# Rotary embedding on one core: casting transfers of every fourth partition with 16 KB rows, and 4,096-wide VectorE operations

## The chip, the cores and the metric

The kernel runs on one core of one Trainium2 chip. Its time is the device time of an execution in microseconds (us); for the kernel before it is 168.24 us, the median of two runs that agree. The profile is of one execution, and its span, from the first to the last instruction, is 166.5 us.

Five kinds of engine matter little or much here: VectorE (DVE in the profile) does all the arithmetic, GpSimd (POOL) issues all large transfers, SyncE (SP) issues two small ones, and the core's 16 DMA engines move the data between the chip's memory (HBM) and the on-chip memory of 128 partitions (SBUF). TensorE and ScalarE do nothing.

## The reference

Each row of 1,024 numbers is cut into 16 heads of 64, and each head into two halves of 32. The halves are rotated by tables that depend on the position in the sequence:

```python
batch, seq, dim = 16, 512, 1024          # x: float32, 33.55 MB
num_heads = 16                           # head_dim = 64, half_dim = 32
x1, x2 = x[..., :half_dim], x[..., half_dim:]
cos = cos[None, :, None, :]              # cos, sin: (512, 32)
sin = sin[None, :, None, :]
rotated = np.concatenate([
    x1 * cos - x2 * sin,
    x1 * sin + x2 * cos,
], axis=-1)                              # float32, 33.55 MB
```

## The kernel before

Each of the 128 partitions holds four neighbouring positions of a batch entry (`spp = 4`). A chunk is two of these positions for all partitions: 128 x 2,048 elements, 8 KB of float32 for each partition. There are 32 chunks. GpSimd's loads cast float32 to bf16 on the way into SBUF, its stores cast bf16 to float32 on the way out.

```python
spp = seq // P                 # 4
rows = 2
W = rows * dim                 # 2048
per_batch = spp // rows        # 2
nchunks = batch * per_batch    # 32
ahead = 6
xpool: bufs=ahead + 3;  tpool: bufs=3;  opool: bufs=6

def dram(t, c):
    b, k = divmod(c, per_batch)
    return bass.AP(tensor=t.tensor,
                   offset=t.offset + b * seq * dim + k * rows * dim,
                   ap=[[spp * dim, P], [1, W]])

def load(c):
    xb = xpool.tile([P, W], bf16, tag="xb")
    nc.gpsimd.dma_start(out=xb, in_=dram(x, c))
    return xb
# ... cos and sin are loaded by SyncE, the first `ahead` chunks by GpSimd;
# ... VectorE makes the bf16 tables cc = [cos, cos] and ss = [sin, -sin]

for c in range(nchunks):
    # ...
    for j in range(rows):          # operations of 1,024 elements
        nc.vector.tensor_mul(out=row(t1), in0=row(xb), in1=tab(cc))
        nc.vector.tensor_mul(out=row(t2), in0=row(xb), in1=tab(ss))
        # swapped: t2 with the two halves of each head exchanged
        nc.vector.tensor_add(out=row(ot), in0=row(t1), in1=swapped)
    nc.gpsimd.dma_start(out=dram(out_flat, c), in_=ot)
    if c + ahead < nchunks:
        xbs[c + ahead] = load(c + ahead)
```

`tab(t)` reads a row of 64 table entries 16 times over, once for each head. In GpSimd's order each store is followed by the load of the chunk six further on.

## Time and profile before

| | |
|---|---|
| Time | 168.24 us |
| Span of the profiled execution | 166.5 us |
| VectorE busy | 120.1 us (72%), 195 instructions |
| GpSimd busy | 34.5 us (21%), 68 instructions |
| Loads issued by GpSimd | 32, each 512 KB as written to SBUF (1 MB as read) |
| Stores issued by GpSimd | 32, each 1,024 KB as written to HBM |
| Mean of one VectorE operation of 1,024 elements | 0.684 to 0.687 us |
| Mean of one DMA issue on GpSimd | 0.538 us |

The profile's page shows, for each engine, how much of the span it was busy, and the same in 40 equal slices, in which a digit 9 stands for 90% or more. A row for the DMA engines stands beside them. The chain of waits starts from the last instruction and steps back, each time to whatever released it, so its shares say what the end of the kernel hung on. The table of groups has one line per kind of instruction: how many, their busy time, the mean duration in ns, and behind the last bar the idle time of the engine just ahead of them and what ended it. VectorE's operations overlap a little: each is 0.68 us long, but one starts every 0.60 us when nothing holds it.

Sizes of transfers are given as written, so a load counts half of what it reads from HBM. The trace also has a record of every packet that a DMA engine handled, with its start, duration and size as written. One row of one partition is one packet.

### The profile page before, as it was taken

The numbers are of one execution on the slowest core, as the hardware profiler recorded it, in microseconds if no ns is written. First come the engines' busy times: TensorE is split into PE (matmuls) and PEld (weight loads), VectorE is DVE, ScalarE is ACT, GpSimd is POOL, SyncE is SP. The second block draws the span as 40 slices with busy tenths as digits, with TensorE's granted clock in tenths as the row PEclk, the third lists the DMA queues.
The fourth block names the chain that finished last, engine by engine and source line by source line (L and its number), as shares of the span: only waits on it lengthen the run. The fifth ranks groups of instructions, "written<-read, shape, count | busy, mean of one in ns | idle before, by whom it ended". The sixth has DMA issues, their size and how long they took to land.

```text
span 166.5 us, 365 instructions
## 1 busy us (share of the span) xinstructions
DVE 120.1 (72%) x195; POOL 34.5 (21%) x68
## 2 busy tenths in 40 slices
DVE  1399999998778878777987777797775987775000
POOL 7123222222212212221221221221221211111000
DMA  4999999999999999999999999999999999999980
GB/s 74 203 217 208 270 299 302 324 341 340 326 303 297 311 334 342 338 312 303 299 322 337 342 333 301 303 302 336 337 340 318 299 303 314 341 371 431 429 333 2
DMA packets 9507, 50.49 MB, mean 303 GB/s; under 512 B 1056, under 2 KB 1312, under 8 KB 5408
## 3 DMA queue, kind: packets, MB, share of 16 engines
q0 software_dynamic: 9216, 50.34, 104.1%
q1 hardware_dynamic: 288, 0.13, 0.3%
q14 instruction: 3, 0.02, 0.0%
HBM read 33.69 MB, written 33.55 MB: 404 GB/s over the span
## 4 chain that ended last, share of the span: by engine, by line
DMA 72%; issue 9%; DVE 9%; POOL 1%; POOLq 0%; DVEq 0%; PEldq 0%
DMA xb<-in_x_dram 72%; DVE t L95 3%; DVE ot L100 3%; DVE t L96 3%; POOL out_dram L101 1%; POOLq L134 0%; POOLq L101 0%; DVEq L95 0%; PEldq L134 0%
## 5 line engine op out<-in xcount | busy, mean ns | idle before, releaser
L95 DVE TENSOR_TENSOR t<-xb,cc 128x1024 bf16<-128x1024 bf16 x64 | 44.0, 687 | 28.8 <-DMA xb<-in_x_dram 28.8
L100 DVE TENSOR_TENSOR ot<-t,t 128x1024 bf16<-128x1024 bf16 x64 | 43.9, 686 | 0.7
L96 DVE TENSOR_TENSOR t<-xb,ss 128x1024 bf16<-128x1024 bf16 x64 | 43.8, 684 | 0.0
L101 POOL DMA_DIRECT2D out_dram<-ot x32 | 17.2, 538 | 85.0 <-DMA out_dram<-ot 42.2
L52 POOL DMA_DIRECT2D xb<-in_x_dram x32 | 17.1, 539 | 33.3 <-DMA xb<-in_x_dram 32.5
L68 DVE CAST cc<-cos_sb 128x256 bf16<-128x256 f32 x1 | 0.3, 294 | 2.6 <-DMA cos_sb<-in_cos_dram 2.6
L76 DVE CAST ss<-sin_sb 128x128 bf16<-128x128 f32 x1 | 0.2, 227 | 0.1
L77 DVE TENSOR_SCALAR ss<-sin_sb 128x128 bf16<-128x128 f32 x1 | 0.2, 220 | 0.0
L120 POOL MEMSET const-float32-0.0<- 128x1 f32 x1 | 0.1, 99 | 0.2 <-issue 0.2
L120 POOL MEMSET const-bfloat16-1.0<- 128x1 bf16 x1 | 0.1, 102 | 0.0
L120 POOL MEMSET const-float32-1.0<- 128x1 f32 x1 | 0.1, 99 | 0.0
L120 POOL MEMSET const-uint8-127<- 128x1 uint8 x1 | 0.1, 99 | 0.0
## 6 DMA issues: line engine op xcount, KB each, us to landing
out_dram<-ot POOLq DMA_DIRECT2D x32, 1024.0 KB, 19.1
xb<-in_x_dram POOLq DMA_DIRECT2D x32, 512.0 KB, 19.3
cos_sb<-in_cos_dram SPq DMA_DIRECT2D x1, 64.0 KB, 1.8
sin_sb<-in_sin_dram SPq DMA_DIRECT2D x1, 64.0 KB, 1.8
```

The lines of the kernel that those rows point to most:

```text
L52: nc.gpsimd.dma_start(out=xb, in_=dram(x, c))
L68: nc.vector.tensor_copy(out=cc, in_=dataclasses.replace(cos_sb, ap=[cos_sb.ap[0], [half, spp], [0, 2], [1, half]]))
L76: nc.vector.tensor_copy(out=ss_half(0), in_=sin_rows)
L77: nc.vector.tensor_scalar_mul(out=ss_half(1), in0=sin_rows, scalar1=-1.0)
L95: nc.vector.tensor_mul(out=row(t1), in0=row(xb), in1=tab(cc))
L96: nc.vector.tensor_mul(out=row(t2), in0=row(xb), in1=tab(ss))
L100: nc.vector.tensor_add(out=row(ot), in0=row(t1), in1=swapped)
L101: nc.gpsimd.dma_start(out=dram(out_flat, c), in_=ot)
L120: nc = _bacc.Bacc("TRN2", target_bir_lowering=False, num_devices=1)
```

## The change

A chunk becomes all four positions of a partition, 128 x 4,096 elements, so a row is 16 KB of float32 and there are 16 chunks. Each chunk is moved by four transfers; transfer `r` takes partitions `r, r+4, r+8, ...`, which are 32 rows. In GpSimd's order, store `r` of a chunk is followed by load `r` of the chunk three further on, so that stores and loads alternate in pieces of 512 KB at the float32 side. Three chunks are loaded ahead, the same number of bytes as six of the chunks before.

VectorE makes both products and the sum of a chunk in one operation each, 4,096 elements wide. The purpose is fewer and larger packets, a finer alternation of loads and stores, and fewer VectorE instructions.

```diff
-    rows = 2
+    rows = 4
     W = rows * dim
     per_batch = spp // rows
     nchunks = batch * per_batch
-    ahead = 6
+    ahead = 3
+    pstep = 4
...
-    xpool = ctx.enter_context(tc.tile_pool(name="xpool", bufs=ahead + 3))
+    xpool = ctx.enter_context(tc.tile_pool(name="xpool", bufs=ahead + 1))
     tpool = ctx.enter_context(tc.tile_pool(name="tpool", bufs=3))
-    opool = ctx.enter_context(tc.tile_pool(name="opool", bufs=6))
+    opool = ctx.enter_context(tc.tile_pool(name="opool", bufs=4))
...
-    def dram(t, c):
+    def dram(t, c, r):
         b, k = divmod(c, per_batch)
         return bass.AP(tensor=t.tensor,
-                       offset=t.offset + b * seq * dim + k * rows * dim,
-                       ap=[[spp * dim, P], [1, W]])
+                       offset=t.offset + b * seq * dim + r * spp * dim + k * W,
+                       ap=[[pstep * spp * dim, P // pstep], [1, W]])
...
+    def load(c, r):
+        if r == 0:
+            xbs[c] = xpool.tile([P, W], bf16, tag="xb", name="xb")
+        nc.gpsimd.dma_start(out=xbs[c][r::pstep, :], in_=dram(x, c, r))
+
+    def store(c, r, ot):
+        nc.gpsimd.dma_start(out=dram(out_flat, c, r), in_=ot[r::pstep, :])
...
+    for c in range(ahead):
+        for r in range(pstep):
+            load(c, r)
...
-            nc.vector.tensor_mul(out=row(t1), in0=row(xb), in1=tab(cc))
-            nc.vector.tensor_mul(out=row(t2), in0=row(xb), in1=tab(ss))
-            swapped = dataclasses.replace(
-                t2, offset=t2.offset + j * dim + half,
-                ap=[t2.ap[0], [hd, nh], [-half, 2], [1, half]])
-            nc.vector.tensor_add(out=row(ot), in0=row(t1), in1=swapped)
-        nc.gpsimd.dma_start(out=dram(out_flat, c), in_=ot)
-        if c + ahead < nchunks:
-            xbs[c + ahead] = load(c + ahead)
+        def tab(t):
+            return view(t, k * rows * hd, (hd, rows), (0, nh), (1, hd))
+
+        nc.vector.tensor_mul(out=t1, in0=xb, in1=tab(cc))
+        nc.vector.tensor_mul(out=t2, in0=xb, in1=tab(ss))
+        nc.vector.tensor_add(
+            out=ot, in0=t1, in1=view(t2, half, (hd, rows * nh), (-half, 2), (1, half)))
+        for r in range(pstep):
+            store(c, r, ot)
+            if c + ahead < nchunks:
+                load(c + ahead, r)
```

The rest of the difference rewrites the making of the tables with a helper (`view`) and leaves the same instructions.

## The prediction

> **What bounds the kernel now.** I read the page's DMA slices first, then the chain of waits, then stretches by window, then the trace's records of single DMA packets.

> ```profile
> DMA  4999999999999999999999999999999999999980
> GB/s 74 203 217 208 270 299 302 324 341 340 326 303 297 311 334 342 338 312 303 299 322 337 342 333 301 303 302 336 337 340 318 299 303 314 341 371 431 429 333 2
> DMA packets 9507, 50.49 MB, mean 303 GB/s; under 512 B 1056, under 2 KB 1312, under 8 KB 5408
> ...
> HBM read 33.69 MB, written 33.55 MB: 404 GB/s over the span
> ```

> The DMA engines are busy in every slice but the first and last two. The GB/s row looks uneven only because it counts a casting load by the 2-byte side that it writes. HBM traffic, both directions, is 67.24 MB: 404 GB/s over the span.

> ```profile
> DMA xb<-in_x_dram 72%; DVE t L95 3%; DVE ot L100 3%; DVE t L96 3%; POOL out_dram L101 1%; POOLq L134 0%; POOLq L101 0%; DVEq L95 0%; PEldq L134 0%
> ...
> L95 DVE TENSOR_TENSOR t<-xb,cc 128x1024 bf16<-128x1024 bf16 x64 | 44.0, 687 | 28.8 <-DMA xb<-in_x_dram 28.8
> L100 DVE TENSOR_TENSOR ot<-t,t 128x1024 bf16<-128x1024 bf16 x64 | 43.9, 686 | 0.7
> ...
> out_dram<-ot POOLq DMA_DIRECT2D x32, 1024.0 KB, 19.1
> xb<-in_x_dram POOLq DMA_DIRECT2D x32, 512.0 KB, 19.3
> ```

> 72% of the chain is a transfer. VectorE's idle time ends with a load. A transfer takes 19 us from issue to landing, because it stands in a queue: the issue at 40.05 us in the chain was released by the landing of the one issued at 22.98, eight transfers earlier. Eight in flight is the depth, before and after (eight completion counters go round).

> The windows separate a stretch with loads alone, one with both, and one with stores alone (columns: stretch, its length, VectorE busy, GpSimd busy, clock, DMA share, GB/s).

> ```profile
> 7.00:19.00 12.00, 11.98 (x20) 2.29 (x5) 1.00 1.06 200
> 36.00:142.00 106.00, 82.46 (x133) 21.90 (x41) 1.00 1.09 319
> 152.50:161.00 8.50, 0.00 (x0) 0.53 (x1) 1.00 1.13 431
> ```

> The first stretch is mostly loads (its end holds the change to stores); in the last, stores run at 431 GB/s with VectorE idle. Between, 319 is what the sum of a load's and a store's time gives: mixing gains and loses nothing.

> The packet records give the price of each part. On one engine in the steady stretch, a load packet (8 KB read, 4 KB written) starts 304.6 ns after the one before it, a store packet (4 KB read, 8 KB written) 303.4 ns, and a 4-byte completion packet at the end of each transfer takes about 21 ns. One load plus one store of 1 MB at the float32 side is 8 x 304.6 + 8 x 303.4 + 2 x 21 = 4,906 ns. Issues of loads in the timeline are 4.91 us apart, so this is the whole period. Per engine the kernel is 256 x 304.6 + 256 x 303.4 + 64 x 21 = 157.0 us of packets; the first data packet starts at 2.63 us, the last ends at 162.76, and 3.7 us follow. **It is bound by the DMA engines' packet time**, VectorE (120.1 us) is not.

> [...] 9,216 packets of this queue less 8,192 rows are 1,024, or 64 transfers x 16. 32 partitions should therefore still use all 16 engines, two rows each. [...]

> **The change part by part.**

> 1. Rows of 16 KB. Same bytes, half the data packets: per engine 128 loads and 128 stores. [...] Sum 154.9 us, against 155.6 before: **0.7 us saved**.

> 2. 128 transfers in place of 64, each on 16 engines: 128 x 21 ns = 2.7 us per engine against 1.3: **1.3 us added**. Parts 1 and 2 together: 157.6 against 157.0, **0.6 us more** on the bounding path.

> 3. GpSimd issues 128 transfers. At the 0.54 us of today's issues (an upper estimate, since each has a quarter of the rows) that is 69 us in all, 4.3 us for the eight issues of one chunk against 9.8 us of packets: hidden.

> 4. VectorE: 48 operations of 4,096 in place of 192 of 1,024. [...] the sum waits for the product just ahead of it, which costs 0.12 more (the tail has 0.72 us between such a pair where 0.60 is usual). About 6.7 us a chunk, 108 us in all against 115.6 (192 x 0.602). It saves 8 us of an engine that waits for loads anyway: 0.

> 5. Longer lead-in. The first chunk is now 2 MB read. In the kernel before, the slowest engine's completion for the second load, the same bytes, is at 9.07 us, and computing follows a landing by 0.41 us: start 9.5, first result 16.2, first store issue 16.3. A first packet follows its issue by up to 1.37 us (1.26 to 2.63 at the start): 17.7. The three chunks ahead are the same bytes as six loads today, and those keep the queue full until the first store packet at 18.95 us. Slack 1.3 us: 0.

> 6. Longer tail. From the last load's landing: 0.41 + 6.7 + 0.04 + 1.37 = 8.5 us until the last stores' first packet. Eight stores stand ahead of them[...]. Engines finish up to 1.2 us apart (most at 161.0 to 161.9 us, one at 162.76), which uses up most of the slack: 0, at worst some tenths on engines that do not end last.

> 7. Depth. Eight in flight are now 9.8 us of packets instead of 19.6. A slot that comes free needs up to about 0.3 + 1.37 us to give data again; seven others hold 8.6 us: 0.

> Sum: 168.24 + 0.6[...]: **168.7 us**.

> **The rivals.**

> (a) *Completions cost nothing extra while 16 KB rows save.* Then part 2 goes away: 157.6 - 2.7 = 154.9 us of packets against 157.0, 2.1 us less, 166.2 us. For it: the completion's 21 ns may partly lie beside the neighbouring packets. Against it: the 4.91 us period needs both completions in the sum.

> (b) *The load and the store overlap now that they alternate in small pieces.* A load reads twice what it writes, a store the other way, so an engine that read ahead could gain much. Against it: at each of today's changes from load to store the next packet starts at the usual 303 to 305 ns, plus the completion; nothing is gained at the seam. Twice as many seams gain twice nothing.

> (c) *The ring runs dry* at lead-in or tail, where I found a slack of about 1.3 us each. If descriptors of the small transfers are slower, or operations cost 0.4 us more, 1 to 3 us are lost: 170 to 172.

> (d) [...] a few per cent at worst, 170 to 175.

> (e) [...] The innermost runs (32 and 64 elements of bf16, step 1) are as before, so I give it 2%.

> **Range and chances.** The change leaves the bytes alone[...]. Faster by over 2%: 0.05. (c), (d), (e) and a costlier completion lie on the slow side: 0.13. Within 2%: 0.82. Range 167.0 to 170.8 us.

> **What would show it.** Step 1: 4,096 data packets, start to start near 605 ns; packets of 303 ns would mean that rows are split. Step 2: 2,048 completion packets of about 21 ns. Steps 3 and 4: issues of at most 0.54 us, operations 2.2 us apart. Steps 5 and 6: no slice of the DMA row below 9 near 18 us or ahead of the last stores. Step 7: GpSimd waiting for landings, with about 9.8 us from issue to landing. The prediction is wrong if the period of eight transfers is not near 9.85 us, or if a gap opens in the ring.

## The result, and the profile after

The changed kernel takes 170.48 us (median of two runs, 170.35 and 170.61) against 168.24 us before: a ratio of 1.0133, 95% interval 1.0089 to 1.0177. It is a little slower, less than 2%, and inside the range of the prediction; but most of what was lost was not in the prediction's sum.

The page of the changed kernel, in the order in which the prediction read that of the kernel before: the DMA rows, the chain, the groups, the issues.

```profile
DMA  5999999999999999999999999999999999999930
GB/s 89 210 210 210 249 334 329 309 315 332 313 303 334 330 307 317 334 307 311 334 330 295 323 332 303 315 340 325 299 321 330 309 313 340 319 420 424 424 136 0
DMA packets 6434, 50.49 MB, mean 299 GB/s; under 512 B 2080, under 2 KB 2336, under 8 KB 2336
...
DMA xb<-in_x_dram 77%; DVE ot L102 3%; DVE t L101 3%; POOL out_dram L66 2%; POOL xb L63 2%; DVE t L100 1%; POOLq L138 0%; DVEq L100 0%; DVEq L102 0%; PEldq L138 0%
...
L100 DVE TENSOR_TENSOR t<-xb,cc 128x4096 bf16<-128x4096 bf16 x16 | 36.7, 2291 | 42.2 <-DMA xb<-in_x_dram 42.2
L66 POOL DMA_DIRECT2D out_dram<-ot x64 | 34.2, 535 | 59.3 <-DMA out_dram<-ot 40.9
L63 POOL DMA_DIRECT2D xb<-in_x_dram x64 | 33.9, 533 | 29.3 <-DMA xb<-in_x_dram 28.5
...
out_dram<-ot POOLq DMA_DIRECT2D x64, 512.0 KB, 9.6
xb<-in_x_dram POOLq DMA_DIRECT2D x64, 256.0 KB, 9.6
```

It is still bound by the DMA engines: no slice between the first and the last two falls below 9, and VectorE waits 42 us for loads. A transfer now takes 9.6 us from issue to landing, half as long as before, with eight in flight and half the bytes in each. But the last slice is empty, and the last but one nearly so. The windows of its end (stretch, length, VectorE, GpSimd, clock, DMA share, GB/s) show how long the DMA engines stand idle before the kernel is over; the kernel before (166.5 us) first, then the changed one (168.6 us):

```profile
162.00:164.00 2.00, 0.00 (x0) 0.00 (x0) 1.00 0.02 8
164.00:166.00 2.00, 0.00 (x0) 0.00 (x0) 1.00 0.00 0
```

```profile
160.00:162.00 2.00, 0.00 (x0) 0.00 (x0) 1.00 0.77 303
162.00:164.00 2.00, 0.00 (x0) 0.00 (x0) 1.00 0.01 0
164.00:166.00 2.00, 0.00 (x0) 0.00 (x0) 1.00 0.00 0
166.00:168.00 2.00, 0.00 (x0) 0.00 (x0) 1.00 0.00 0
```

The last data packet ends at 162.24 us, half a microsecond *earlier* than in the kernel before (162.76). What runs in the empty stretch is no arithmetic and no transfer. It is a drain instruction on GpSimd, which stands behind the last line of every kernel here. The line of the closing code, asked for alone, has it (number of instructions, shortest, median and longest duration in ns, first and last start); the kernel before first, then the changed one:

```profile
L134 POOLq DRAIN  x3: 45/96/13254, 152.5 to 166.2; - x3
```

```profile
L138 POOLq DRAIN  x3: 45/96/11689, 156.2 to 168.3; - x3
```

The longest drain starts with the last issue and so covers the time in which the last stores still run. Its end counts: 152.50 + 13.25 = 165.75 us before, 156.17 + 11.69 = 167.86 after. In the packet records the last completion packet starts at 162.72 and 162.20. So the drain goes on for **3.03 us** behind the last completion before, and for **5.66 us** after. I call this the closing gap.

The spans differ by 168.59 - 166.49 = 2.10 us, and this is where it lies:

| Part | us |
|---|---|
| Mean start of the last 16 completion packets, one on each engine: 161.57 before, 161.71 after | +0.14 |
| Slowest engine behind that mean (the last of the 16): 1.15 before, 0.49 after | -0.66 |
| Closing gap: 3.03 before, 5.66 after | +2.63 |
| Sum | +2.11 |

### The profile page after: what moved, and what is told of

Same layout as the page of the kernel before. It is cut to its first block, busy times and chain, and to the rows that moved or that the text cites. A ratio compares the mean times of both kernels' runs of the same rounds, so it can differ in the third digit from the quotient of the medians.

```text
span 168.6 us, 299 instructions
## 1 busy us (share of the span) xinstructions
DVE 109.1 (65%) x51; POOL 68.2 (40%) x132
## 2 busy tenths in 40 slices
DMA packets 6434, 50.49 MB, mean 299 GB/s; under 512 B 2080, under 2 KB 2336, under 8 KB 2336
## 3 DMA queue, kind: packets, MB, share of 16 engines
HBM read 33.69 MB, written 33.55 MB: 399 GB/s over the span
## 4 chain that ended last, share of the span: by engine, by line
DMA 77%; DVE 7%; POOL 4%; issue 4%; POOLq 0%; DVEq 0%; PEldq 0%
DMA xb<-in_x_dram 77%; DVE ot L102 3%; DVE t L101 3%; POOL out_dram L66 2%; POOL xb L63 2%; DVE t L100 1%; POOLq L138 0%; DVEq L100 0%; DVEq L102 0%; PEldq L138 0%
## 5 line engine op out<-in xcount | busy, mean ns | idle before, releaser
L100 DVE TENSOR_TENSOR t<-xb,cc 128x4096 bf16<-128x4096 bf16 x16 | 36.7, 2291 | 42.2 <-DMA xb<-in_x_dram 42.2
L66 POOL DMA_DIRECT2D out_dram<-ot x64 | 34.2, 535 | 59.3 <-DMA out_dram<-ot 40.9
L63 POOL DMA_DIRECT2D xb<-in_x_dram x64 | 33.9, 533 | 29.3 <-DMA xb<-in_x_dram 28.5
L102 DVE TENSOR_TENSOR ot<-t,t 128x4096 bf16<-128x4096 bf16 x16 | 36.7, 2292 | 0.6
L101 DVE TENSOR_TENSOR t<-xb,ss 128x4096 bf16<-128x4096 bf16 x16 | 36.6, 2285 | 0.0
## 6 DMA issues: line engine op xcount, KB each, us to landing
out_dram<-ot POOLq DMA_DIRECT2D x64, 512.0 KB, 9.6
```

The costliest lines, as they stand in the source:

```text
L63: nc.gpsimd.dma_start(out=xbs[c][r::pstep, :], in_=dram(x, c, r))
L66: nc.gpsimd.dma_start(out=dram(out_flat, c, r), in_=ot[r::pstep, :])
L100: nc.vector.tensor_mul(out=t1, in0=xb, in1=tab(cc))
L101: nc.vector.tensor_mul(out=t2, in0=xb, in1=tab(ss))
L102: nc.vector.tensor_add(out=ot, in0=t1, in1=view(t2, half, (hd, rows * nh), (-half, 2), (1, half)))
```

## The experiments

Theory A: the time of the transfers is the sum of packets and completions as predicted, and the closing gap grows with the number of transfers that GpSimd issued, by about 41 ns each ((5.66 - 3.03) / 64). Theory B: the gap comes with 16 KB rows. Theory C: it comes with late, large or strided transfers, or the fine alternation matters in another way. Unless it is said otherwise, times are medians beside runs of the kernel before on the same chip (168.07 to 168.19 us).

**One, two transfers a chunk.** The edit is in the changed kernel (and 2 in place of 1 for the second run):

```diff
-    pstep = 4
+    pstep = 1
```

> The changed kernel with each chunk moved by one transfer of all 128 partitions (32 transfers in place of 128; rows stay 16 KB, VectorE unchanged). Theory A (each transfer costs 21 ns on every DMA engine for its completion, and about 41 ns at the end[...]): the gap from the last completion packet to the end of the drain falls from 5.6 to about 1.3 to 1.7 us, packets fall by 96 x 21 ns = 2.0 us, time 164.6 us. Rival B (the longer closing belongs to the 16 KB rows, not to the number of transfers): the gap stays near 5.6 us, time 168.5. Rival C (the fine alternation of loads and stores or every fourth partition brings something that the rest hides): time over 168.5.

> The changed kernel with two transfers a chunk, every second partition (64 transfers, 16 KB rows). Theory A: closing gap 3.0 us as in the kernel before, packets 64 x 21 ns = 1.3 us less, time 166.5 us. Rival B: gap 5.6 us, time 169.1.

With one transfer a chunk: 165.03 us, ratio 0.9821 (0.9806 to 0.9835), closing gap 1.73 us. Its drain, from 153.46 us, ends at 162.31, and the last completion packet starts at 160.58:

```profile
L138 POOLq DRAIN  x3: 39/93/8852, 153.5 to 162.8; - x3
```

With two: 167.46 us, ratio 0.9953 (0.9936 to 0.9970), gap 3.03 us. B is out: the rows are 16 KB in both, and the gap of the second is that of the kernel before. C finds nothing for itself: 32 coarse transfers are faster than 128 fine ones. The mean last completion of the first run is at 159.92 us, 1.8 us ahead of the changed kernel's, where 96 x 21 ns = 2.0 us was expected. In this run five loads of a whole chunk stand ahead of the first store, where the changed kernel has three chunks, so its lead-in is not quite the same.

The second run has as many transfers as the kernel before, with rows of 16 KB in place of 8 KB, and so gives the price of the rows by themselves: between 16 and 48 MB of float32 traffic its completions are 78.17 us apart, those of the kernel before 78.53. That is 0.36 us for half of the data, or 0.7 us for all of it, as the first part of the prediction had it.

The second run is 1.0 us above what was expected. Its windows near the end show a part of this: the ring (the queue of packets at the DMA engines) is not full there. The DMA share can go above 1, since the records of neighbouring packets overlap a little (a row of 16 KB is recorded with about 625 ns and the next starts after 605).

```profile
152.00:154.00 2.00, 1.97 (x2) 0.00 (x0) 1.00 1.04 418
154.00:156.00 2.00, 0.71 (x1) 0.99 (x2) 1.00 0.70 279
156.00:158.00 2.00, 0.00 (x0) 0.08 (x1) 1.00 1.20 492
```

0.70 where its neighbours have 1.04 and 1.20, just as the last two stores are issued: the tail's slack, which the prediction put close to nothing, was used up in this one.

**More transfers with the old rows.** In the kernel before, each load and each store becomes two of every second partition:

```diff
-        nc.gpsimd.dma_start(out=xb, in_=dram(x, c))
+        for r in range(2):
+            nc.gpsimd.dma_start(out=xb[r::2, :], in_=dram(x, c, r))
...
-        nc.gpsimd.dma_start(out=dram(out_flat, c), in_=ot)
+        for r in range(2):
+            nc.gpsimd.dma_start(out=dram(out_flat, c, r), in_=ot[r::2, :])
```

> The kernel before with each transfer cut into two of every second partition (128 transfers, rows of 8 KB as before). Theory A: closing gap 5.6 us, packets 1.3 us more, time 172.2 us. Rival B: gap 3.0 us, time 169.6.

171.79 us, ratio 1.0235 (1.0208 to 1.0261), closing gap 5.66 us with rows of 8 KB. The mean last completion moved from 161.57 to 162.94 us, by 1.37: the 64 x 21 ns = 1.34 us of the added completions. The steady stretch tells the same: 79.23 us between 16 and 48 MB against 78.53, or 1.4 us for all of the data. This run has both losses, completions and closing gap, with the old rows, and so separates them from the rows.

**Adjacent partitions.** The changed kernel with four blocks of 32 partitions; if transfers of adjacent partitions were slower, their packets would stand further apart:

```diff
-        nc.gpsimd.dma_start(out=xbs[c][r::pstep, :], in_=dram(x, c, r))
+        nc.gpsimd.dma_start(out=xbs[c][r * 32:(r + 1) * 32, :], in_=dram(x, c, r))
```

(and the same in the store and in the addresses of `dram`)

> The changed kernel with blocks of 32 adjacent partitions in place of every fourth. Theory A says nothing of it beyond the same closing gap, 5.6 us. [...] if the DMA engines' own rate bounds, 170.5 us.

171.35 us, ratio 1.0200 (1.0177 to 1.0223), gap 5.66 us. Between 16 and 48 MB of float32 traffic the completions of both versions are equally far apart (78.86 against 78.84 us), so adjacent partitions cost nothing there. The profiled run is 1.1 us longer than the changed kernel's: 0.3 in the lead-in, 0.4 between 48 MB and the end, and 0.3 because its slowest engine ends 0.83 us behind the mean, not 0.49. The cause of all three stays open.

**VectorE's part alone.** The kernel before with three operations of 2,048 elements in place of six of 1,024:

```diff
-        for j in range(rows):
-            # ... three operations on 1,024 elements
+        nc.vector.tensor_mul(out=t1, in0=xb, in1=tab(cc))
+        nc.vector.tensor_mul(out=t2, in0=xb, in1=tab(ss))
+        nc.vector.tensor_add(out=ot, in0=t1, in1=view(t2, half, (hd, rows * nh), (-half, 2), (1, half)))
```

> The kernel before with VectorE's part of the change alone: three operations of 2,048 elements a chunk in place of six of 1,024; transfers untouched. If VectorE is off the path: the same time, 168.1 us within 0.5, although its busy time falls by 5 us or more. If the wide operations themselves delay something (first store later, in-order waits): over 169.

167.69 us, ratio 0.9969 (0.9957 to 0.9982): the 0.5 us at the edge of what "off the path" allowed. Its runs spread from 167.51 to 168.24, and the profiled one was the slowest, with a gap of 3.04 us and its last data packet at 162.74 as in the kernel before. So the wide operations cost nothing; where the half microsecond of the other runs comes from, no profile here shows.

**The closing gap by itself.** In the version with 32 transfers, 96 small loads stand ahead of the first load. They go into memory that nothing reads. In the second run SyncE issues them, in the third GpSimd drains once behind them:

```diff
+    scr = singles.tile([P, 96 * 128], f32, tag="scr")
+    for i in range(96):
+        nc.gpsimd.dma_start(out=scr[0:16, i * 128:(i + 1) * 128], in_=...)   # 16 rows of 512 B
+    nc.gpsimd.drain()                                                        # third run only
     for c in range(ahead):
```

> The version with 32 transfers, and ahead of its first load 96 more small ones from GpSimd (16 rows of 512 B each, into memory that nothing reads): 128 transfers issued by GpSimd. It is slower by the time that these take at the start; what counts is the gap at the end. Theory A: 0.43 + 128 x 0.041 = 5.7 us, though these 96 landed more than 100 us earlier and are tiny. Rivals (the gap belongs to large, late or strided transfers): 1.7 us.

> The same 96 small transfers, issued by SyncE in place of GpSimd. If the closing gap counts the transfers that GpSimd issued: 1.7 us. If it counts all transfers of the core: 5.7 us.

> The kernel with 96 small transfers from GpSimd at its start, and right behind these a drain instruction on GpSimd of its own, ahead of the first load. If the closing drain works off what was issued since the last drain: the early drain takes about 4 us, and the closing gap is 0.43 + 32 x 0.041 = 1.7 us. If each drain pays for all that was issued so far: the early one takes 4 us too, but the closing gap stays 5.7 us.

One execution each. With GpSimd: gap **5.67 us**, that of the changed kernel, though the 96 were tiny and had landed more than 100 us before the end. With SyncE: **1.74 us**. With the drain between: **1.75 us**. So the gap counts what GpSimd issued since its last drain, whatever the size, and not what SyncE issued. (Their times, 214.2, 168.1 and 218.6 us, contain the small loads and say nothing more.) The early drain went on for 7.0 us behind the last small completion, where I expected about 4. So the 41 ns for each transfer hold for the drains at the end of these kernels, not for every drain; why stays open.

**More of the same.** The changed kernel with eight transfers a chunk (`pstep = 8`), one execution:

> The changed kernel with eight transfers a chunk, every eighth partition, one 16 KB row on each DMA engine (256 transfers). Theory A: closing gap 0.43 + 256 x 0.041 = 10.9 us; completions 2.7 us more on each engine than with 128; together 170.5 + 5.2 + 2.7 = 178.4 us if eight transfers in flight (4.9 us of packets) still keep the ring full, more if not.

172.3 us, not 178.4, and the closing gap is not 10.9 but **1.00 us**: the last drain starts at 165.51 us and ends at 169.80, the last completion packet starts at 168.81.

```profile
L138 POOLq DRAIN  x3: 45/96/4293, 165.5 to 170.3; - x3
```

Theory A in its first form fails here. The run's table of waits (who waited for what, us, times, longest) and its timeline (start, duration, idle time and its end in brackets) show what happens instead:

```profile
POOL out_dram L66 <- issue: 23.9, 81, 3.1
```

```profile
80.35 0.48 POOL L63 DMA_DIRECT2D xb<-in_x_dram  x1
83.96 0.49 POOL L66 DMA_DIRECT2D out_dram<-ot  x1 [3.13 <-issue]
84.44 0.49 POOL L63 DMA_DIRECT2D xb<-in_x_dram  x1
```

GpSimd stands still for 3.13 us, waiting for nothing that the profile shows, exactly ahead of its 129th transfer, and once more for 2.87 us ahead of its 250th. Theory D, a count made to fit this run: the closing gap goes by a count of GpSimd's transfers that does not keep all of them. At a count of 128 GpSimd stops ahead of the next transfer, and 121 go off the count, with seven taken as still in flight. 121 + 128 = 249, which fits the second stop. 256 - 242 = 14 are left at the close: 0.43 + 14 x 0.041 = 1.00 us, as measured. What GpSimd does in the stop, no trace shows. By D the changed kernel is the worst case: it ends with a count of 128, ahead of any stop.

The stops are not free here. Eight transfers in flight are about 5 us of packets (one takes 4.7 us from issue to landing), and behind each stop the ring runs empty:

```profile
84.00:86.00 2.00, 1.97 (x2) 2.00 (x5) 1.00 0.74 180
162.00:164.00 2.00, 0.00 (x0) 0.99 (x3) 1.00 0.05 16
```

By the packet records the data falls behind its steady pace by about 1.8 us at the first stop and 2.2 at the second. With 2.7 us of completions more and 4.7 us of closing gap less than in the changed kernel, this makes the time up: 2.7 + 4.0 - 4.7 = 2.0 us more, and the measured spans are 170.54 and 168.59 us.

**A test of D.** A kernel with *more* transfers than the changed one should have the shorter close:

```diff
-    pstep = 4
+    def step(c):
+        return 8 if c < 3 else 4
```

> The changed kernel with eight transfers each way for the first three chunks and four for the rest: 152 transfers. Theory D, from the run with 256[...]: a stop of 3.1 us ahead of the 129th issue, beside transfers that still run, then a closing gap of 0.43 + 31 x 0.041 = 1.7 us; completions add 24 x 21 ns = 0.5 us; time 167.0 us, faster than with 128 although there are more transfers. Theory A as first stated (41 ns at the end for every transfer of the run): gap 6.7 us, time 172.0 us.

The timeline of GpSimd around its 129th transfer:

```profile
126.25 0.53 POOL L65 DMA_DIRECT2D xb<-in_x_dram  x1 [0.67 <-DMA xb<-in_x_dram]
130.44 0.53 POOL L68 DMA_DIRECT2D out_dram<-ot  x1 [3.67 <-issue]
130.97 0.53 POOL L65 DMA_DIRECT2D xb<-in_x_dram  x1
```

The stop is there, at this transfer, 3.67 us with the usual wait for a free slot in it, and the closing gap is **1.70 us** as D has it (152 - 121 = 31 are counted). The time is 168.61 us (ratio to before 1.0027, 1.0013 to 1.0041): faster than the changed kernel by 1.9 us, with 24 transfers more. It is 1.6 us above the 167.0 expected, and the DMA windows of its lead-in say where: 0.98, 0.87, 1.05 and 0.92 from 2 to 10 us.

```profile
4.00:6.00 2.00, 0.00 (x0) 2.00 (x5) 1.00 0.87 131
6.00:8.00 2.00, 0.00 (x0) 0.75 (x2) 1.00 1.05 164
8.00:10.00 2.00, 0.00 (x0) 1.15 (x4) 1.00 0.92 184
```

131 to 184 GB/s, where the changed kernel's loads reach 201 to 213 from 4 to 12 us: with transfers of one row on each engine the ring is not full at the start. Why is open: eight in flight cannot be the whole reason, since GpSimd issues the first ten without a wait, until 6.3 us. By the time that 8 MB had moved, the profiled run of this version, which took 169.18 us, was 2.1 us behind that of the changed one. During the stop itself the ring stayed full (1.04 from 128 to 130 us): eight transfers of this size are 9.8 us of packets.

**The version that follows from it.** Below 128, fewer transfers were cheaper in every run so far, so one transfer takes two batch entries, except at the two ends:

```diff
+    loads = [1, 1, 2, 2, 2, 2, 2, 2, 2]      # batch entries in each load
+    stores = [2, 2, 2, 2, 2, 2, 2, 1, 1]
...
+    ap=[[spp * dim, P], [seq * dim, n], [1, W]]
```

(The buffers change with it: eight batch entries are loaded ahead of the first store.)

> One transfer for two batch entries (two 16 KB rows a partition), except for the first two loads and the last two stores: 18 transfers on GpSimd in all, VectorE as in the changed kernel. Theory A (21 ns of completion on each engine and 41 ns of closing drain for each transfer): closing gap 0.43 + 18 x 0.041 = 1.2 us against 1.7 with 32 transfers, completions 0.3 us less, time 164.2 us. Rival (coarser pieces leave a gap in the ring at the lead-in or the tail): 165 to 170.

**164.14 us**, ratio 0.9757 (0.9743 to 0.9772), closing gap 1.19 us. Its page:

```profile
DMA  4999999999999999999999999999999999999992
HBM read 33.69 MB, written 33.55 MB: 414 GB/s over the span
```

The DMA engines now work to within the last slice, and the same bytes as before go through at 414 GB/s over the span in place of 404. This beats both kernels.

The closing gaps together, with the rule 0.43 us + 41 ns for each transfer of GpSimd that is counted at the close. The 41 ns are (5.66 - 3.03) / 64, and the 0.43 makes the rule fit the first runs. The rows with 18 and 152 transfers and those with small ones were forecast with the rule before they ran; the 14 of the last row was worked out afterwards.

| Run | GpSimd transfers, counted at the close | Rule, us | Measured, us |
|---|---|---|---|
| Two batch entries a transfer | 18, 18 | 1.17 | 1.19 |
| One transfer a chunk | 32, 32 | 1.74 | 1.73 |
| The same with 96 from SyncE | 32, 32 | 1.74 | 1.74 |
| Kernel before | 64, 64 | 3.05 | 3.03 |
| Two transfers a chunk | 64, 64 | 3.05 | 3.03 |
| Changed kernel | 128, 128 | 5.68 | 5.66 |
| Before, each transfer cut in two | 128, 128 | 5.68 | 5.66 |
| 96 small ones first | 128, 128 | 5.68 | 5.67 |
| The same, drained behind them | 128, 32 | 1.74 | 1.75 |
| Eight for three chunks | 152, 31 | 1.70 | 1.70 |
| Eight transfers a chunk | 256, 14 | 1.00 | 1.00 |

## Why the prediction was right, and where it was wrong

The direction and the range held: 170.48 in 167.0 to 170.8. The point, 168.7, was 1.8 us short, and the reason is one term of the sum. That the range held is in part luck: the term that failed cost 2.6 us and was not among the rivals, and a part of it was hidden by about 0.9 us of gains that the prediction did not have either. Without these the time would have been about 171.4 us.

**The term that failed**: "the last ends at 162.76, and 3.7 us follow". The prediction carried these 3.7 us over as a constant. They are not: 3.03 of them are the closing gap, which nearly doubled, to 5.66, with the number of transfers; behind the last data packet 6.4 us followed. The page shows nothing of it in its groups, since a drain is not counted as busy (the busy tenths of line L134 are all 0), but the chain of the kernel before ended on GpSimd's own queue (its last entry is the closing line), and the question of what those 3.7 us depend on could have been asked.

**Step 1, rows of 16 KB: right.** 2,048 packets each way. From one row of a load to the next, and from its last row to its completion packet, are 605 to 606 ns. A store's second row starts 586 ns after the first and is followed by its completion after 603 to 604; the load behind that starts 41 ns later instead of 21. Together these are 1,231 ns. With 21 ns of that for the completion, a store's row is 605 ns, and all rows are 128 x 605.5 + 128 x 605 = 154.9 us. The prediction's 154.9 was an estimate, and these packets bear it out. The run with two transfers a chunk has the 0.7 us by itself.

**Step 2, completions: right.** 2,048 of them, 16 for each of the 128 transfers as before. Eight transfers take 9.849 us in the steady stretch (issues at 29.84 and 138.18 us, eleven periods); the prediction named "near 9.85". From 16 MB to the end the mean completion lost 0.42 us against the kernel before, of the 0.6 predicted for the whole run. The run with each old transfer cut in two gave the 21 ns by themselves (about 1.4 us for 64).

**Step 3, hidden issues: right on the path, wrong in detail.** 0.53 us a transfer, not less for a quarter of the rows; 68 us in all, hidden.

**Step 4, VectorE: right.** The first chunk's products and sum run from 9.13 to 15.95 us, 6.8 where the prediction had 6.7, an estimate. It is off the path; the run with VectorE's part alone gained 0.3%, which the prediction had as 0.

**Steps 5 and 6, lead-in and tail: no gap, as predicted, and a gain that I missed.** The first store was issued at 16.25 us (16.3 predicted). By 16 MB the mean completion was 0.28 us ahead of the kernel before (43.50 against 43.78), and the slowest engine fell 0.49 us behind the mean instead of 1.15. These two hid about 0.9 us of the 2.6 of the closing gap. Why the engines end closer together no run here tells. In the kernel before they end 1.5 us apart, from 161.19 to 162.72, rather than the 1.2 of step 6, which is the slowest one's distance from the mean. The point of 168.7 is 0.1 us below 168.24 + 0.6, an estimate for the lead-in; the first data packet starts at 2.60 us against 2.63.

**Step 7, depth: right** for this kernel. With transfers of half the size the steady pace still held (16 of them, from 59.75 to 69.76 us, take 10.01 us, which is the 9.85 and eight more completions), but the ring ran empty behind GpSimd's stops.

**The rivals.** (a) is out: 64 more completions took about 1.4 us. (b) is out: twice the seams, no gain (78.84 us between 16 and 48 MB against 78.53). (c) did not happen here, but it did a little at the end of the run with two transfers a chunk. (d), a loss from the partitions that a transfer takes, did not show in the steady stretch even with adjacent ones (78.86 us against 78.84). (e), slower operations with the added table dimension, did not happen: they follow each other every 2.21 us (2.32 into the sum).

## What to carry to other kernels

In a kernel that the DMA engines bound, look at what happens behind the last packet, too: here each transfer issued by GpSimd, up to 128 of them, cost 21 ns on every DMA engine and another 41 ns at the very end. Cutting transfers into smaller ones for a finer alternation pays both and gains nothing where a load and a store already take the sum of their times. Make GpSimd's transfers as large as the lead-in and the tail allow: from 128 to 18 transfers the same data took 164.1 us instead of 170.5.
